# New start addresses for TensorE's operands, and single 256-column matmuls in the last SwiGLU stage

## The chip, the cores and the metric

The kernel runs on one core of a Trainium2 chip. The metric is the device time of one execution in microseconds (us), the median of several runs. TensorE (PE in the profile) multiplies; its weight loads are shown as PEld. VectorE is DVE, ScalarE is ACT, GpSimd is POOL, SyncE (SP) issues the large DMAs.

## The reference: what is computed

Sixteen meta tokens are put ahead of 256 tokens, so T = 272 rows of width D = 2048. Two layers follow, all in float32.

```python
h = concat([meta, x])                                             # 272 x 2048
h = h + short_conv_mixer(rms_norm(h), a_w_in, a_conv, a_w_out)    # 2048 -> 3*2048 -> 2048
h = h + swiglu(rms_norm(h), w_gu[0], w_down[0])                   # 2048 -> 2*5632, 5632 -> 2048
k, v, c = shared_kv(h, w_kv, w_f)                                 # keys, values, forget gate
h = h + forgetting_attention(rms_norm(h), w_q, w_o, k, v, c)      # 16 heads of 128
h = h + swiglu(rms_norm(h), w_gu[1], w_down[1])
return h[16:]                                                     # the meta rows are dropped
```

After the keys and values the meta rows are no longer needed, so from the queries on only the 256 real columns are computed.

## The kernel before, in words

The activations are kept transposed: 128 features in the partitions, the 272 (or 256) tokens along the columns. They are TensorE's **moving** operand. The weights are its stationary operand: every matmul of a 128 x 128 block of a weight matrix is preceded by the load of that block.

**Split operands.** Each float32 operand is split into two float32r parts, hi (the rounded value) and lo (the rest). A product of a weight block and an activation block is three matmuls into one PSUM accumulator: hi weights with the hi part, hi weights with the lo part, lo weights with the hi part (`mm3`, lines 101 to 103). Each of them has its own weight load.

**Slabs.** All weights stream through one list of slabs. A slab is 128 x 1024 float32 (512 KB): SP loads it into one of four `raw` buffers (line 86), ScalarE makes `whi` from it (line 95), VectorE `wlo` (line 96), each with four buffers, and TensorE then does the eight products of the slab. The main loop at the end of the kernel issues for slab i its matmuls, the split of slab i + 3, and the work that follows on finished accumulators. A slab is loaded once.

**Stages in order.** The gated convolution layer and the first SwiGLU use 272 columns (`ALL`). The attention stage mixes k and v projections (272 columns, moving operand `x`), q projections (256 columns, operands `bh` and `bl`), the work of each head (k times q, p times v, small norms, transposes) and the output projection `add_wo` (256 columns, `hid`). The last SwiGLU uses 256 columns (`REAL`).

**The last SwiGLU.** There `halves` is true (line 443): hi and lo of the moving operand lie side by side, and `product` (lines 105 to 116) does two matmuls instead of three. One has 512 columns (hi weights with hi and lo together, lines 113 and 116), the other 256 (lo weights with hi, line 114, added to the second half of the bank). The two halves of the accumulator are summed afterwards: `half_sum` by one copy on ScalarE (line 291) and one addition on VectorE (line 292), `add_residual_halves` by a copy on ScalarE (line 302), an addition on VectorE (line 303) and one on GpSimd (line 304). In the last eight blocks of products (`plain` = 14) three matmuls of 256 are used even before.

**Where operands begin.** SBUF tiles follow each other in the pools in the order in which the code makes them. What counts here is the byte address at which an operand begins, modulo 256. In the memory map of the built kernel before:

| operand | starts, bytes modulo 256 |
|---|---|
| weight buffers `raw`, `whi`, `wlo` (each 128 x 128 block is 512 bytes further) | 96 |
| `x`, `hid` with 272 columns: hi, lo | 192, 0 |
| `x`, `hid` with 256 columns: hi, lo | 224, 224 |
| `bh`, `bl` (q projection) | 224, 224 |
| p times v: moving `phi`, `plo`; weights `vhi`, `vlo` | 160; 96 |
| head norms: moving `sqh`, `sql`; weights `onesr` | 224 or 32, 96 or 160; 128 |
| k times q: moving `khi`, `klo`; weights `qhi`, `qlo` | 224 or 32, 96 or 160; 224 |

The gate of the attention stage (`gate_mm`) has the moving operands of `x` with 272 columns, and weights of 16 columns in place of 128, which begin at 224, 32, 96 and 160 in turn.

Of the kernel before, what the change touches and what calls it, by code (L numbers as in the profile page):

```python
# [9 lines left out]
F32 = mybir.dt.float32  # L10
F32R = mybir.dt.float32r
# [4 lines left out]
P = 128  # L16
NM = 16
S = 256
T = NM + S
D = 2048  # L20
KT = D // P
# [9 lines left out]
RAW_BUFS = 4  # L31
SPLIT_BUFS = 4
XROW = 640
XPAD = 24
XB = 72


@with_exitstack
def kernel(ctx, tc, x, meta, a_norm, a_w_in, a_conv, a_w_out, kv_norm, w_kv,
# [3 lines left out]
    V, A, G, PE = nc.vector, nc.scalar, nc.gpsimd, nc.tensor  # L43

    const = ctx.enter_context(tc.tile_pool(name="const", bufs=1))
    wpool = ctx.enter_context(tc.tile_pool(name="wpool", bufs=1))
    xpool = ctx.enter_context(tc.tile_pool(name="xpool", bufs=1))
    work = ctx.enter_context(tc.tile_pool(name="work", bufs=1))
    psum = ctx.enter_context(tc.tile_pool(name="psum", bufs=8, space=bass.MemoryType.PSUM))
    dram = ctx.enter_context(tc.tile_pool(name="dram", bufs=1, space=bass.MemoryType.DRAM))  # L50

    uid, late, pp = [0], [], []
    LATE = {f"b{c}{k}" for c in "hl" for k in range(KT)}
    LATE |= {"khi", "klo", "vhi", "vlo", "qhi", "qlo", "pst", "vst", "v3", "c3", "bias", "ck", "sqh", "sql"}

    def nm(s):
        uid[0] += 1
        return f"{s}_{uid[0]}"

    def wt(tag, shape, dt=F32, bufs=1):  # L60
        pool = late[0] if tag in LATE else work
        return pool.tile(shape, dt, tag=tag, name=nm(tag), bufs=bufs)

    def ps(tag):
        return psum.tile([P, 512], F32, tag="ps", name=nm(tag), bufs=8)
# [110 lines left out]
    def add_down(w, row, xs, cols, post, plain=16):  # L176

        first = None
        for pnl in range(4):
            src = w[row:row + 512, pnl * 512:(pnl + 1) * 512].rearrange("(k p) c -> p k c", p=P)  # L180
            accs = {}

            def mk(s, accs=accs, pnl=pnl):
                def mm(hi, lo):
                    for m in range(2):
                        xl = [x if pnl * 4 + s * 2 + m < plain else x[:2] + (None,) for x in xs()]
                        acc = accs[s, m] = ps("acc")
                        for k in range(4):
                            product(acc, cols, hi[:, k, m * P:(m + 1) * P],
                                    lo[:, k, m * P:(m + 1) * P], xl[k], k == 0, k == 3)  # L190
                return mm

            def mkpost(s, accs=accs, pnl=pnl):
                return lambda: [post(pnl * 4 + s * 2 + m, accs[s, m]) for m in range(2)]

            i = add_panel(src, "b", [mk(0), mk(1)], [[mkpost(0)], [mkpost(1)]])
            if first is None:
                first = i
        return first
# [4 lines left out]

    ident = const.tile([P, P], F32, name="ident")
    make_identity(nc, ident)
    ones = const.tile([P, P], F32, name="ones")
    G.memset(ones, 1.0)
    onesr = const.tile([P, P], F32R, name="onesr")
    G.tensor_copy(onesr, ones)  # L210
    epsb = const.tile([P, 1], F32, name="epsb")
    G.memset(epsb, EPS)
    small = const.tile([P, 4], F32, name="small")
# [7 lines left out]
    A.activation(warm, ones[:, 0:1], AF.Copy)  # L221


    xpool.tile([P, XPAD], F32R, name="xpad")
    state = {}

    def make_operand(key, src, gain, cols):

        k = len(state[key])
        n = cols.stop - cols.start  # L230
        at = XB if n == S else 0
        both = xpool.tile([P, XROW], F32R, tag=f"x{k}", name=nm(f"x{k}"))[:, at:]
        hi, lo = both[:, 0:n], both[:, n:2 * n]
        A.activation(hi, src, AF.Copy, scale=gain)
        V.scalar_tensor_tensor(out=lo, in0=src, scalar=gain, in1=hi.bitcast(F32),
                               op0=ALU.mult, op1=ALU.subtract)
        state[key].append((hi, lo, both[:, 0:2 * n] if 2 * n <= 512 else None))

    def add_square(k, src, cols, pool=False):
        if k == 0:  # L240
# [32 lines left out]
    def new_hidden():  # L273
        return xpool.tile([P, 4, XROW], F32R, tag="hid", name=nm("hid"), bufs=2)

    def hidden_parts(hid, k, n):
        at = XB if n == S else 0
        return hid[:, k, at:at + n], hid[:, k, at + n:at + 2 * n]

    def put_hidden(hid, k, src, n):  # L280

# [2 lines left out]
        V.tensor_tensor(out=lo, in0=src, in1=hi.bitcast(F32), op=ALU.subtract)  # L284

    def hidden_view(hid, n, both=False):
        return [hidden_parts(hid, k, n) + (hid[:, k, XB:XB + 2 * n] if both else None,) for k in range(4)]

    def half_sum(acc):
        t = wt("u", [P, T + 2], bufs=3)[:, 0:S]  # L290
        A.activation(t, acc[:, S:2 * S], AF.Copy)
        V.tensor_tensor(out=t, in0=acc[:, 0:S], in1=t, op=ALU.add)
        return t
# [64 lines left out]

    def start_done():
        start.__exit__(None, None, None)  # L360
        late.append(ctx.enter_context(tc.tile_pool(name="late", bufs=1)))
        pp.extend(late[0].tile([P, 512], F32R, name=t) for t in ("phi", "plo"))
        for t in pp:
            G.memset(t[:, 0:P].bitcast(F32), 0.0)
        G.dma_start(small[:, 0:1], k_norm.rearrange("(p o) -> p o", o=1))
        G.dma_start(small[:, 1:2], b_q_norm.rearrange("o p -> p o"))
        G.dma_start(small[0:H, 2:3], b_f.rearrange("(p o) -> p o", o=1))
        state["wf"] = wt("ck", [P, T])[:, 0:KT * H].rearrange("p (k c) -> p k c", k=KT)
        G.dma_start(state["wf"], w_f.rearrange("(k p) c -> p k c", p=P))
# [56 lines left out]
    def make_xb(m):  # L426
        if m == 0:
            state["xb"] = []
        hi = wt(f"bh{m}", [P, S], F32R)
        lo = wt(f"bl{m}", [P, S], F32R)  # L430
        t = wt("bias", [P, P + NM + T], bufs=2)[:, 0:S]
        gain = gcol[:, BN + m:BN + m + 1]
        A.activation(t, h[m][:, REAL], AF.Copy, scale=gain)
        A.activation(hi, t, AF.Copy)
        G.tensor_tensor(out=lo, in0=t, in1=hi.bitcast(F32), op=ALU.subtract)
        state["xb"].append((hi, lo, None))


    def ffn_phase(layer, cols, after):
        gu, dn = ffn_w_gu[layer], ffn_w_down[layer]  # L440
        nch = FT // 4
        n = cols.stop - cols.start
        halves = 2 * n <= 512
        plain = 14
        hid = {}
        xkey, rkey = f"xf{layer}", f"rf{layer}"
        for c in range(nch):
            col, uu = c * 512, {}

            def post_g(m, acc, uu=uu):  # L450
                r = state[rkey][:, cols]
                g = half_sum(acc) if halves else acc[:, cols]
                gs = wt("tmpa", [P, T], bufs=2)[:, 0:n]
                V.tensor_tensor(out=gs, in0=g, in1=r, op=ALU.mult)
                th = wt("tmpb", [P, T], bufs=2)[:, 0:n]
                A.activation(th, gs, AF.Tanh, scale=0.5)
                a = wt(("cs", "sc")[m // 2], [P, T], bufs=2)[:, 0:n]
                V.scalar_tensor_tensor(out=a, in0=th, scalar=1.0, in1=gs,  # L458
                                       op0=ALU.add, op1=ALU.mult)
                G.tensor_tensor(out=a, in0=a, in1=r, op=ALU.mult)  # L460
                uu[m] = a

            def post_u(m, acc, uu=uu, c=c):
                if m == 0:
                    hid[c] = new_hidden()
                u = half_sum(acc) if halves else acc[:, cols]
                z = wt("cv", [P, T], bufs=2)[:, 0:n]
                V.scalar_tensor_tensor(out=z, in0=uu[m], scalar=0.5, in1=u,
                                       op0=ALU.mult, op1=ALU.mult)
                put_hidden(hid[c], m, z, n)  # L470

            xs = lambda: state[xkey]
            if c == 0:
                hook(len(slabs) + 2, lambda: norm_stats(rkey, cols))
            add_up4(gu, col, xs, cols, post_g)
            add_up4(gu, F + col, xs, cols, post_u)
            for cc in ([c - 1] if 0 < c < nch - 1 else [c - 1, c] if c else []):
                def post_o(m, acc, cc=cc):
                    if halves and (cc < nch - 1 or m < plain):
                        add_residual_halves(m, acc, cc == nch - 1 and m >= plain - 2)  # L480
                    else:
                        add_residual(m, acc, cols)
                    if cc == nch - 1:
                        after(m)
                i = add_down(dn, cc * 512, lambda cc=cc: hidden_view(hid[cc], n, halves), cols,
                             post_o, plain if cc == nch - 1 else 16)
        return i

# [270 lines left out]
    i = ffn_phase(1, REAL, final_post)  # L759
# [52 lines left out]
```

## Time and profile before

| | |
|---|---|
| median of 3 runs | 2374.8 us (2374.6 to 2375.61) |
| the profiled execution, its own time | 2375.75 us |
| its span, first to last instruction | 2374.0 us |
| granted TensorE clock | 1.000 of full speed (2.4 GHz) |
| DMA, mean | 177 GB/s |

The profile counts an engine as busy while an instruction of it is under way. Matmuls overlap in their pipeline: a matmul of 272 columns is under way for some 288 ns, while the next one starts much sooner. What a matmul costs in a dense stream is therefore the step from its start to the next start, not its duration. In a stretch of the trace the step is the length of the stretch by the number of matmuls in it.

### The profile page before, as it was taken

Reading aid. Unit: us, or ns where it says so; the run is one execution under the profiler, and the core shown is the slowest. Engines: PE = TensorE matmul, PEld = TensorE weight load, DVE = VectorE, ACT = ScalarE, POOL = GpSimd, SP = SyncE. Lnnn points to the kernel's source line nnn. Section 1 sums busy time; section 2 is a strip of 40 time slices with the busy share of each in tenths; the row PEclk is TensorE's granted clock in tenths of the full one; section 3 lists DMA queues with packets and bytes.
Section 4 is the critical chain, followed back from the end, with each engine's and each line's share of the span. In section 5 each row is a group of like instructions: output and inputs, shape, how many; then the busy total and the mean of one; then the engine's idle time right before and its main releaser. Section 6 shows DMA issues by size and latency. Waiting matters only on the chain.

```text
span 2374.0 us, 43349 instructions
## 1 busy us (share of the span) xinstructions
PE 2366.6 (100%) x17266; PEld 2263.3 (95%) x17266; DVE 1596.4 (67%) x2350; ACT 1169.1 (49%) x1800; POOL 505.7 (21%) x585
## 2 busy tenths in 40 slices
PE   9999999999999999999999999999999999999999
PEld 8999999999999999999999999999888888888888
DVE  6665668656556566556788666778667767766677
ACT  5443345433333333333567565666555555555555
POOL 4110113000000000000265232423123223322233
PEclk9999999999999999999999999999999999999999
DMA  6555555555555555555555545545555565555554
GB/s 213 176 177 178 178 177 175 172 178 177 178 178 178 175 176 176 177 177 178 169 165 163 166 155 170 161 154 177 187 187 189 183 194 188 184 189 187 187 190 147
DMA packets 418555, 420.63 MB, mean 177 GB/s; under 512 B 13217, under 2 KB 416769, under 8 KB 418337
## 3 DMA queue, kind: packets, MB, share of 16 engines
q1 hardware_dynamic: 417280, 415.43, 54.8%
q0 software_dynamic: 1072, 2.44, 0.4%
q8 instruction: 136, 2.23, 0.4%
q14 instruction: 67, 0.54, 0.1%
HBM read 415.70 MB, written 2.11 MB: 176 GB/s over the span
## 4 chain that ended last, share of the span: by engine, by line
PE 99%; DMA 0%; DVE 0%; ACT 0%; SPq 0%; POOL 0%; issue 0%; ACTq 0%; DVEq 0%
PE acc L101 22%; PE acc L103 22%; PE acc L102 21%; PE acc L116 18%; PE acc L114 11%; PE acc L113 3%; PE aux L103 0%; PE aux L101 0%; PE aux L102 0%; PE aux L345 0%; PE aux L657 0%; PE aux L677 0%; DMA m<-in_meta_dram 0%; PE aux L546 0%; PE aux L547 0%; PE aux L750 0%
## 5 line engine op out<-in xcount | busy, mean ns | idle before, releaser
L96 DVE TENSOR_TENSOR wlo<-raw,whi 128x1024 fp32r<-128x1024 f32 x784 | 1019.6, 1301 | 646.6 <-ACT whi L95 643.2
L95 ACT ACTIVATE whi<-raw 128x1024 fp32r<-128x1024 f32 x784 | 829.4, 1058 | 917.3 <-PE acc L102 655.9
L101 PE MATMUL acc<-x,whi 128*128 128x272 f32 x2688 | 780.0, 290 | 0.0
L103 PE MATMUL acc<-x,wlo 128*128 128x272 f32 x2688 | 773.5, 288 | 0.0
L102 PE MATMUL acc<-x,whi 128*128 128x272 f32 x2688 | 772.5, 287 | 0.0
L103 PEld LDWEIGHTS acc<-x,wlo 128*128 128x128 f32 x2688 | 511.1, 190 | 0.0
L101 PEld LDWEIGHTS acc<-x,whi 128*128 128x128 f32 x2688 | 506.1, 188 | 1.4 <-ACT whi L95 0.3
L102 PEld LDWEIGHTS acc<-x,whi 128*128 128x128 f32 x2688 | 506.4, 188 | 0.1
L116 PE MATMUL acc<-x,whi 128*128 128x512 f32 x1320 | 467.1, 393 | 0.0
L114 PE MATMUL acc<-x,wlo 128*128 128x256 f32 x1408 | 383.4, 282 | 0.0
L101 PE MATMUL acc<-hid,whi 128*128 128x272 f32 (+1 forms) x1224 | 351.9, 288 | 0.0
L103 PE MATMUL acc<-hid,wlo 128*128 128x272 f32 (+1 forms) x1224 | 350.4, 286 | 0.0
L102 PE MATMUL acc<-hid,whi 128*128 128x272 f32 (+1 forms) x1224 | 349.7, 286 | 0.0
L116 PEld LDWEIGHTS acc<-x,whi 128*128 128x128 f32 x1320 | 247.9, 188 | 53.8
L114 PEld LDWEIGHTS acc<-x,wlo 128*128 128x128 f32 x1408 | 264.7, 188 | 7.6
L103 PEld LDWEIGHTS acc<-hid,wlo 128*128 128x128 f32 x1224 | 232.1, 190 | 0.1
L102 PEld LDWEIGHTS acc<-hid,whi 128*128 128x128 f32 x1224 | 230.3, 188 | 0.0
L101 PEld LDWEIGHTS acc<-hid,whi 128*128 128x128 f32 x1224 | 230.1, 188 | 0.0
L460 POOL TENSOR_TENSOR cs<-cs,rstd 128x272 f32<-128x272 f32 (+1 forms) x44 | 33.3, 757 | 899.6 <-DVE cs L458 899.6
L304 POOL TENSOR_TENSOR h<-h,u 128x256 f32<-128x256 f32 x172 | 156.3, 934 | 269.0 <-DVE h L303 269.0
L116 PE MATMUL acc<-hid,whi 128*128 128x512 f32 x522 | 190.6, 394 | 0.0
L114 PE MATMUL acc<-hid,wlo 128*128 128x256 f32 x696 | 167.7, 281 | 0.0
(194 smaller groups left out, 2379.3 us busy)
## 6 DMA issues: line engine op xcount, KB each, us to landing
raw<-in_ffn_w_gu_dram SPq DMA_DIRECT2D x352, 512.0 KB, 3.5
raw<-in_ffn_w_down_dram SPq DMA_DIRECT2D x176, 512.0 KB, 3.3
raw<-in_a_w_in_dram SPq DMA_DIRECT2D x96, 512.0 KB, 3.6
raw<-in_w_kv_dram SPq DMA_DIRECT2D x64, 512.0 KB, 3.7
raw<-in_a_w_out_dram SPq DMA_DIRECT2D x32, 512.0 KB, 4.4
raw<-in_b_w_q_dram SPq DMA_DIRECT2D x32, 512.0 KB, 3.3
raw<-in_b_w_o_dram SPq DMA_DIRECT2D x32, 512.0 KB, 3.3
ck<-cdram POOLq DMA_DIRECT2D x16, 136.0 KB, 3.9
```

The costliest lines, as they stand in the source:

```text
L95: A.activation(hi, part, AF.Copy)
L96: V.tensor_tensor(out=lo, in0=part, in1=hi.bitcast(F32), op=ALU.subtract)
L101: PE.matmul(acc, whi, xhi, start=first, stop=False)
L102: PE.matmul(acc, whi, xlo, start=False, stop=False)
L103: PE.matmul(acc, wlo, xhi, start=False, stop=last)
L113: PE.matmul(acc, whi, both, start=True, stop=False)
L114: PE.matmul(acc[:, S:2 * S], wlo, xhi, start=False, stop=False)
L116: PE.matmul(acc, whi, both, start=False, stop=last)
L304: G.tensor_tensor(out=h[m][:, REAL], in0=h[m][:, REAL], in1=t, op=ALU.add)
L460: G.tensor_tensor(out=a, in0=a, in1=r, op=ALU.mult)
```

## The change

It moves operands in SBUF and takes the 512-column matmuls away.

```diff
-XPAD = 24
-XB = 72
+XLO = 320
+WPAD, XPAD, BPAD = 40, 48, 8
...
+    wpool.tile([P, WPAD], F32, name="wpad")
+    xpool.tile([P, XPAD], F32R, name="xpad")
...
-    ones = const.tile([P, P], F32, name="ones")
+    onesr = const.tile([P, P], F32R, name="onesr")
+    ones = onesr.bitcast(F32)
     G.memset(ones, 1.0)
-    onesr = const.tile([P, P], F32R, name="onesr")
-    G.tensor_copy(onesr, ones)
...
+    def halves(n):
+
+        return False
...
-        at = XB if n == S else 0
-        both = xpool.tile([P, XROW], F32R, tag=f"x{k}", name=nm(f"x{k}"))[:, at:]
-        hi, lo = both[:, 0:n], both[:, n:2 * n]
+        both = xpool.tile([P, XROW], F32R, tag=f"x{k}", name=nm(f"x{k}"))
+        at = S if halves(n) else XLO
+        hi, lo = both[:, 0:n], both[:, at:at + n]
...
     def hidden_parts(hid, k, n):
-        at = XB if n == S else 0
-        return hid[:, k, at:at + n], hid[:, k, at + n:at + 2 * n]
+        at = S if halves(n) else XLO
+        return hid[:, k, 0:n], hid[:, k, at:at + n]
...
+        bpool.append(ctx.enter_context(tc.tile_pool(name="bpool", bufs=1)))
+        bpool[0].tile([P, BPAD], F32R, name="bpad")
...
-        hi = wt(f"bh{m}", [P, S], F32R)
-        lo = wt(f"bl{m}", [P, S], F32R)
+        hi, lo = (bpool[0].tile([P, S], F32R, tag=f"b{c}{m}", name=nm(f"b{c}{m}")) for c in "hl")
...
-        halves = 2 * n <= 512
+        pair = halves(n)
...
-                g = half_sum(acc) if halves else acc[:, cols]
+                g = half_sum(acc) if pair else acc[:, cols]
```

The same replacement of `halves` by `pair` (now always false) is made in `post_u`, in `post_o` and in the views of `hid`. By the sizes in the code the starts become, modulo 256: the constants lose one tile of 512 bytes, `wpad` adds 160 bytes to 96, so the weight buffers begin at 0; the twelve buffers take 49,152 bytes, a multiple of 256, and `xpad` adds 192; rows of 640 elements are 2,560 bytes and lo begins 1,280 bytes behind hi, both multiples of 256. So `x`, `hid`, `bh`, `bl`, `phi` and `plo` all begin at 192. The operands of the heads move to multiples of 64: `khi` 0 or 64, `klo` 128 or 192, `qhi` and `qlo` 0, `vhi` and `vlo` 128, `sqh` 0 or 64, `sql` 128 or 192; `onesr` stays at 128.

## Rows read from the trace of the kernel before

**Rows 1.** Page, part 1: busy us (share of the span) xinstructions, whole execution.

```profile
PE 2366.6 (100%) x17266; PEld 2263.3 (95%) x17266; DVE 1596.4 (67%) x2350; ACT 1169.1 (49%) x1800; POOL 505.7 (21%) x585
```

**Rows 2.** Page, part 4: chain of waits that ended last, by engine.

```profile
PE 99%; DMA 0%; DVE 0%; ACT 0%; SPq 0%; POOL 0%; issue 0%; ACTq 0%; DVEq 0%
```

**Rows 3.** Windows: first SwiGLU, last SwiGLU, the start. Busy us (xinstructions), PEclk, DMA, GB/s.

```profile
core 0: us, PE busy (x) PEld busy (x) DVE busy (x) ACT busy (x) POOL busy (x), PEclk, DMA share, GB/s
430.00:1190.00 760.00, 760.00 (x6109) 760.00 (x6108) 461.54 (x607) 309.76 (x377) 48.76 (x57) 1.00 0.55 176
1650.00:2350.00 700.00, 700.00 (x3992) 612.36 (x3991) 497.09 (x669) 370.10 (x584) 190.63 (x205) 1.00 0.59 188
5.00:43.00 38.00, 36.64 (x245) 33.37 (x245) 24.65 (x37) 24.55 (x48) 22.38 (x27) 1.00 0.76 239
```

**Rows 4.** Windows of the last SwiGLU: instructions of line 116, then of line 113.

```profile
1650.00:2350.00 700.00, 623.56 (x1748) 328.05 (x1748) 1.00 0.59 188
...
1650.00:2350.00 700.00, 97.76 (x247) 46.31 (x247) 1.00 0.59 188
```

**Rows 5.** Groups by line and form, PE, whole execution: xcount, busy us, mean ns.

```profile
L101 PE MATMUL acc<-x,whi 128*128 128x272 f32 x2688 | 780.0, 290 | 0.0
...
L116 PE MATMUL acc<-x,whi 128*128 128x512 f32 x1320 | 467.1, 393 | 0.0
...
L101 PE MATMUL acc<-hid,whi 128*128 128x272 f32 x960 | 277.4, 289 | 0.0
...
L116 PE MATMUL acc<-hid,whi 128*128 128x512 f32 x522 | 190.6, 394 | 0.0
...
L101 PE MATMUL acc<-hid,whi 128*128 128x256 f32 x264 | 74.5, 284 | 0.0
...
L101 PE MATMUL acc<-bh,whi 128*128 128x256 f32 x256 | 72.6, 284 | 0.0
...
L113 PE MATMUL acc<-hid,whi 128*128 128x512 f32 x174 | 69.2, 398 | 0.0
L113 PE MATMUL acc<-x,whi 128*128 128x512 f32 x88 | 34.8, 395 | 0.0
```

**Rows 6.** Timeline, merged, line 101 in an output projection: durations min/median/max, first and last start.

```profile
L101 PE MATMUL acc<-hid,whi x64: 279/281/285, 1318.2 to 1340.6; 128*128 128x256 f32 x64
```

**Rows 7.** Timeline of PE in the gate's matmuls: start us, us; the first and the 22nd.

```profile
1223.10 0.29 PE L101 MATMUL aux<-x,sqh 128*16 128x272 f32 x1
...
1225.71 0.29 PE L101 MATMUL aux<-x,sqh 128*16 128x272 f32 x1
```

**Rows 8.** Timeline of PE, p times v of one head: first and last of six.

```profile
1266.94 0.28 PE L101 MATMUL aux<-phi,vhi 128*128 128x256 f32 x1
...
1267.53 0.28 PE L103 MATMUL aux<-phi,vlo 128*128 128x256 f32 x1
```

**Rows 9.** Timeline of PE at head norms: each matmul and the one behind it.

```profile
1311.76 0.28 PE L546 MATMUL aux<-sqh,onesr 128*128 128x256 f32 x1
1311.87 0.28 PE L547 MATMUL aux<-sql,onesr 128*128 128x256 f32 x1
...
1361.34 0.28 PE L546 MATMUL aux<-sqh,onesr 128*128 128x272 f32 x1
1361.46 0.28 PE L101 MATMUL acc<-bh,whi 128*128 128x256 f32 x1
...
1362.17 0.30 PE L547 MATMUL aux<-sql,onesr 128*128 128x272 f32 x1
1362.31 0.28 PE L101 MATMUL acc<-bh,whi 128*128 128x256 f32 x1
```

**Rows 10.** Groups by line, 1650 to 2350 us: busy us, mean ns, idle before and its releaser.

```profile
L304 POOL TENSOR_TENSOR h<-h,u 128x256 f32<-128x256 f32 x162 | 149.1, 946 | 260.6 <-DVE h L303 260.6
...
L302 ACT ACTIVATE u<-acc 128x256 f32<-128x256 f32 x164 | 63.1, 385 | 84.5 <-PE acc L116 79.7
...
L291 ACT ACTIVATE u<-acc 128x256 f32<-128x256 f32 x84 | 32.2, 383 | 41.1 <-PE acc L116 41.1
```

**Rows 11.** Chain of waits in order of time: the longest piece at the start.

```profile
1.74 4.84 DMA m<-in_meta_dram
```

More of the change, by code (lines that the diff above doesn't have):

```diff
@@ L48 @@
     work = ctx.enter_context(tc.tile_pool(name="work", bufs=1))
+    wpool.tile([P, WPAD], F32, name="wpad")
+    xpool.tile([P, XPAD], F32R, name="xpad")
     psum = ctx.enter_context(tc.tile_pool(name="psum", bufs=8, space=bass.MemoryType.PSUM))
     dram = ctx.enter_context(tc.tile_pool(name="dram", bufs=1, space=bass.MemoryType.DRAM))
-    uid, late, pp = [0], [], []
-    LATE = {f"b{c}{k}" for c in "hl" for k in range(KT)}
-    LATE |= {"khi", "klo", "vhi", "vlo", "qhi", "qlo", "pst", "vst", "v3", "c3", "bias", "ck", "sqh", "sql"}
+    uid, late, pp, bpool = [0], [], [], []
+    LATE = {"khi", "klo", "vhi", "vlo", "qhi", "qlo", "pst", "vst", "v3", "c3", "bias", "ck", "sqh", "sql"}
     def nm(s):
@@ L221 @@
     A.activation(warm, ones[:, 0:1], AF.Copy)
-    xpool.tile([P, XPAD], F32R, name="xpad")
     state = {}
+    def halves(n):
+        return False
     def make_operand(key, src, gain, cols):
@@ L236, in make_operand @@
                                op0=ALU.mult, op1=ALU.subtract)
-        state[key].append((hi, lo, both[:, 0:2 * n] if 2 * n <= 512 else None))
+        state[key].append((hi, lo, both[:, 0:2 * n] if halves(n) else None))
     def add_square(k, src, cols, pool=False):
@@ L286, in hidden_view @@
     def hidden_view(hid, n, both=False):
-        return [hidden_parts(hid, k, n) + (hid[:, k, XB:XB + 2 * n] if both else None,) for k in range(4)]
+        return [hidden_parts(hid, k, n) + (hid[:, k, 0:2 * n] if both else None,) for k in range(4)]
     def half_sum(acc):
@@ L465, in post_u @@
                     hid[c] = new_hidden()
-                u = half_sum(acc) if halves else acc[:, cols]
+                u = half_sum(acc) if pair else acc[:, cols]
                 z = wt("cv", [P, T], bufs=2)[:, 0:n]
@@ L478, in post_o @@
                 def post_o(m, acc, cc=cc):
-                    if halves and (cc < nch - 1 or m < plain):
+                    if pair and (cc < nch - 1 or m < plain):
                         add_residual_halves(m, acc, cc == nch - 1 and m >= plain - 2)
@@ L484, in post_o @@
                         after(m)
-                i = add_down(dn, cc * 512, lambda cc=cc: hidden_view(hid[cc], n, halves), cols,
+                i = add_down(dn, cc * 512, lambda cc=cc: hidden_view(hid[cc], n, pair), cols,
                              post_o, plain if cc == nch - 1 else 16)
```

## The prediction, on record before the changed kernel ran

> **What bounds the kernel now.** I read the page's busy times first: PE is under way for 2366.6 us of a 2374.0 us span, the next engine, DVE, for 67% of it [rows 1]. A busy PE need not be a PE that sets the end, so the chain of waits comes second: it lies 99% on PE [rows 2]. The windows of the two SwiGLU stages come third: PE is busy in every microsecond, at a granted clock of 1.00 (the upper level, 2.4 GHz), while DVE, ACT and DMA have a quarter or more to spare [rows 3]. So the time is a number of matmuls by the step from one start to the next, and only what changes the count or the step matters.
>
> The steps. In the first SwiGLU 6,109 matmuls touch 760 us; one lasts 290 ns [rows 5], so two had begun before, and 760 us / 6,107 is **124.4 ns** for 272 columns. At one column per cycle of 2.4 GHz it would be 113.3, so 11.1 ns are lost at each. In the output projection 63 triples of 256 columns take 1318.2 to 1340.6 us [rows 6]: 22.4 us / 189 is **118.5 ns**, against 106.7 (11.8 lost). In the last SwiGLU 700 us hold 1,748 + 247 = 1,995 products [rows 4]: **350.9 ns** for a 512 and a 256. The losses add up to about a tenth of the kernel, and the change can only work on them.
>
> **The change part by part.** Its parts are the new starts for the 272-column stages, the same for the 256-column matmuls of attention, two matmuls turned into three in the last SwiGLU, and what falls away on other engines.
>
> *What the starts can do.* The trace has no pair of a moving operand at 192 and weights at 0, so I bound the step from both sides by the same shapes at other starts. At 256 columns the six matmuls of p times v (moving 160, weights 96) go from 1266.94 to 1267.53 in five steps, 118.0 ns each [rows 8]. A head norm (moving 32, next weights at 128) steps 0.11 us [rows 9]; that stamp is good to 0.01, and I read it as 112 to 116. At 272 columns one norm matmul (moving 32, next weights at 96, which is 192 modulo 256 behind, the distance that the change gives everywhere) steps 0.12 us and another (moving 160, next weights 96) 0.14 [rows 9]. So starts do move the step, by several ns and in both directions. What speaks for little at 272 is the gate: its weights have 16 columns in place of 128, and 21 steps from 1223.10 to 1225.71 still take 124.3 ns [rows 7]. If weight reads in the way of moving reads made the whole loss, an eighth of the weights should have made less of it.
>
> *272 columns.* The count is 3 x (2,688 + 960) = 10,944 [rows 5]. Bounds of the new step: 120 below, 132 above (the 0.12 and the low side of 0.14, rounded). I take 123.2, about a quarter of the way from 124.4 to 120: nearest to the thousands of matmuls of the stage and to the gate, a little down for the one row with the distance of the change. 10,944 x 1.2 = **-13.1 us**.
>
> *256 columns in attention.* 3 x (256 + 264) less 24 in the last blocks of the last SwiGLU is 1,536 [rows 5]. Bounds 112 and 122 (the same 3.5 above as the norm lies below its 118.5 at 115). I take 116, between p times v and the norm. 1,536 x 2.5 = **-3.8 us**.
>
> *The last SwiGLU.* 1,320 + 522 + 174 + 88 = 2,104 products [rows 5] go from 350.9 ns to three matmuls of 256. At 116 that is 348.0, so 2,104 x 2.9 = **-6.1 us**; at the step of today it would be 355.5 and a loss of 9.7 us; at the bounds 336 (-31 us) and 366 (+32 us). The break-even is 117.0 ns. The added weight load per product is hidden under the matmul before it as the others are: in the first SwiGLU as many loads as matmuls run at 124.4 ns a step [rows 3].
>
> *What falls away.* In 700 us of that stage the copies on ACT take 63.1 + 32.2 us and the additions on POOL 149.1 us [rows 10]; one DVE addition per block remains. All of it runs beside a PE that is busy throughout [rows 3], so it is costed at nothing; were PE not the cover, it would be a relief and no price. The copy of the ones at the start goes too; there the kernel waits 4.84 us for the meta tokens [rows 11], so nothing again. No wait, no DMA and no step of the order is added: the `b` tiles only lie in a pool of their own. Slabs are used up to 1% sooner, 188 GB/s becoming about 190, while the start moved 239 [rows 3]; DMA stays hidden.
>
> *The sum.* -13.1 - 3.8 - 6.1 = -23.0 us against the profiled execution's own 2375.75 us (1.75 us of it lie outside the span) gives 2352.8; that execution is 0.95 us over the median of the runs shown, so I say **2351.8 us**, and 2335 to 2365 if this reading is right.
>
> **The rivals.**
>
> *Much more comes back* (2286 us). If 192 against 0 keeps the two streams of reads out of each other's way for a whole matmul, 272 columns go at 120 and 256 at 112: -10,944 x 4.4 - 1,536 x 6.5 - 2,104 x (350.9 - 336.0) = -48 - 10 - 31 = -89. For it: these steps do occur [rows 9], and after the change every matmul has the same pair of starts, so a good pair is good 17,000 times. Against it: they occur singly, and the gate's step with short weights is no shorter than the stage's [rows 7].
>
> *Starts make no difference* (2384.5 us, **slower**). Then 272 and 256 columns keep their steps and only the split of the 512s is left: 2,104 x (3 x 118.5 - 350.9) = +9.7 us. It decides as soon as the new 256-column step is over 117.0 ns. For it: the gate, and p times v with another start at 118.0 [rows 7, 8]. Against it: the 0.11 and 0.14 us of the norms [rows 9].
>
> Beside this rival stands a rule: the Trainium skill, SBUF — State Buffer, section "Who interferes with whom", gives PE two independent read ports, one for the moving operand and one for weights, and says that PE never waits on anyone. By that rule starts have no effect and this rival is the outcome; the trace agrees with it in the gate and disagrees in the norms. Another page, TensorE: Matmul & The Clock Gate, section "Back-to-back issue gap", has columns by 2.4 plus 2.5 ns, which is 109.2 for 256 columns and 215.8 for 512; by it three matmuls against a 512 and a 256 would cost 2.6 ns more per product, an estimate of +5 us. The trace has 118.5 where it says 109.2, so the rule lacks a loss of some 9 ns.
>
> *The pair is a bad one* (about 2460 us, slower). The same regularity can hurt: where 272 columns at 160 are followed by weights at 96, the step is 0.14 us [rows 9]; at 132 for all of them, 10,944 x 7.6 = +83 us. One row shows it, at another distance than the change makes.
>
> *The change does not do what it says* only in small: the operands of the heads get multiples of 64, not 192 and 0. They are under 2% of the matmuls.
>
> **How the numbers follow.** About 0.2% (4.7 us) is what a measurement of this kernel can tell from no change. I give my forecast 0.48, the larger gain 0.19, starts without effect 0.18, the bad pair 0.06, and 0.09 to a small gain at 272 columns that the split of the 512s eats up (within 0.2%). Faster is 0.48 + 0.19 = 0.67, same 0.09, slower 0.18 + 0.06 = 0.24. The range reaches from 2290 (most of the larger gain) to 2388 (starts without effect, and 3 us of an uneven step beside it); it leaves out the bad pair and about half of the larger gain.
>
> **What would show it.** Right: in the first SwiGLU about 6,170 matmuls in 760 us instead of 6,109; in the output projection 63 triples in 21.9 us instead of 22.4; in the last SwiGLU about 2,010 products in 700 us, each of three matmuls, with POOL's busy time there down by about 149 us and no gap on PE. Wrong: an unchanged 124.4 ns at 272 columns (then the loss isn't one of starts), a step over 117.0 at 256 (then the split of the 512s costs), or PE waiting for `whi`, `wlo` or a free accumulator in the last stage (then another engine has become the bound).

## The result, and the profile after

The changed kernel takes **2335.6 us** (2334.88 to 2336.14, 4 runs) against 2375.2 us before (2374.6 to 2376.09, 4 runs): ratio 0.9833, 95% interval 0.9816 to 0.985. It is 39.6 us faster. The forecast was 2351.8, so the direction holds, the size was too small, and the time lies inside the range.

The page of the changed kernel, busy times, then the chain of waits by engine:

```profile
PE 2326.6 (100%) x19370; PEld 2315.8 (99%) x19370; DVE 1525.6 (65%) x2260; ACT 1085.4 (46%) x1540; POOL 352.8 (15%) x412
...
PE 97%; DVE 1%; issue 1%; POOL 1%; DMA 0%; ACT 0%; SPq 0%; POOLq 0%; ACTq 0%
```

PE still sets the end, with 2,104 matmuls more than before [rows 1, 2] in 40 us less. So the step from start to start has become shorter. Windows of the changed kernel, first and last SwiGLU (busy us with the number of instructions, by engine):

```profile
430.00:1190.00 760.00, 760.00 (x6162) 759.92 (x6162) 469.57 (x617) 317.72 (x392) 57.08 (x63) 1.00 0.55 178
1650.00:2300.00 650.00, 650.00 (x5738) 650.00 (x5737) 410.49 (x561) 279.63 (x324) 39.95 (x40) 1.00 0.61 194
```

Of the matmuls that touch a window, two had begun before it. At 272 columns the step is 760 us / 6,160 = **123.4 ns** (124.4 before [rows 3]). At 256 columns it is 650 us / 5,736 = **113.3 ns**, so a product of three is 340.0 ns against 350.9 for a 512 and a 256 before [rows 4]. POOL's work in the stage has shrunk from 190.63 us in 700 [rows 3] to 40 in 650, and PE has no gap before or after: that work was indeed beside the path. The granted clock is 1.00 in both kernels.

The output projection of the changed kernel, the timeline merged for line 102 (the first of the three matmuls; line 101 before), says something else:

```profile
L102 PE MATMUL acc<-hid,whi x64: 278/281/281, 1306.5 to 1328.7; 128*128 128x256 f32 x64
```

Here 63 triples take 22.2 us, 117.5 ns a matmul, hardly less than the 118.5 before [rows 6]. It has the same width, the same starts and the same lines of code as the last SwiGLU, and a step that is 4 ns longer. The experiments come back to this.

All steps from one start to the next, added up by stage, give where the time went. The last SwiGLU behind its norm went from 734.1 to 710.9 us (-23.2). The matmuls of 272 columns in all stages take 12.4 us less, and the 256s of attention some 5 (119.9 to 116.8 ns on average, with the steps around other work in between). Together that is about the 40 us.

### The profile page after: what moved, and what is told of

The parts are those of the page before. It is cut to its first block, busy times and chain, and to the rows that moved or that the text cites. A ratio compares the mean times of both kernels' runs of the same rounds, so it can differ in the third digit from the quotient of the medians.

```text
span 2334.4 us, 46907 instructions
## 1 busy us (share of the span) xinstructions
PE 2326.6 (100%) x19370; PEld 2315.8 (99%) x19370; DVE 1525.6 (65%) x2260; ACT 1085.4 (46%) x1540; POOL 352.8 (15%) x412
## 4 chain that ended last, share of the span: by engine, by line
PE 97%; DVE 1%; issue 1%; POOL 1%; DMA 0%; ACT 0%; SPq 0%; POOLq 0%; ACTq 0%
PE acc L102 31%; PE acc L104 31%; PE acc L103 31%; PE aux L104 0%; PE aux L103 0%; PE aux L348 0%; PE aux L102 0%; DVE wlo L97 0%; PE aux L661 0%; DVE x L238 0%; PE aux L681 0%; DMA m<-in_meta_dram 0%; POOL cv L562 0%; PE aux L754 0%; PE aux L663 0%
## 5 line engine op out<-in xcount | busy, mean ns | idle before, releaser
L102 PE MATMUL acc<-x,whi 128*128 128x272 f32 (+1 forms) x4096 | 1162.2, 284 | 0.0
L103 PE MATMUL acc<-x,whi 128*128 128x272 f32 (+1 forms) x4096 | 1160.0, 283 | 0.0
L104 PE MATMUL acc<-x,wlo 128*128 128x272 f32 (+1 forms) x4096 | 1159.6, 283 | 0.0
L102 PEld LDWEIGHTS acc<-x,whi 128*128 128x128 f32 x4096 | 771.5, 188 | 1.4 <-ACT whi L96 0.3
L103 PEld LDWEIGHTS acc<-x,whi 128*128 128x128 f32 x4096 | 771.4, 188 | 0.1
L102 PE MATMUL acc<-hid,whi 128*128 128x272 f32 (+1 forms) x1920 | 541.3, 282 | 0.0
L104 PE MATMUL acc<-hid,wlo 128*128 128x272 f32 (+1 forms) x1920 | 540.8, 282 | 0.0
L103 PE MATMUL acc<-hid,whi 128*128 128x272 f32 (+1 forms) x1920 | 540.7, 282 | 0.0
L102 PEld LDWEIGHTS acc<-hid,whi 128*128 128x128 f32 x1920 | 361.5, 188 | 0.0
L104 PEld LDWEIGHTS acc<-hid,wlo 128*128 128x128 f32 x1920 | 361.1, 188 | 0.1
L103 PEld LDWEIGHTS acc<-hid,whi 128*128 128x128 f32 x1920 | 361.1, 188 | 0.0
L310 DVE TENSOR_TENSOR h<-h,acc 128x272 f32<-128x272 f32 (+1 forms) x480 | 203.0, 424 | 66.1 <-PE acc L104 62.1
L102 PE MATMUL acc<-bh,whi 128*128 128x256 f32 x256 | 71.8, 281 | 0.0
L103 PE MATMUL acc<-bl,whi 128*128 128x256 f32 x256 | 71.1, 278 | 0.0
```

The costliest lines, as they stand in the source:

```text
L102: PE.matmul(acc, whi, xhi, start=first, stop=False)
L103: PE.matmul(acc, whi, xlo, start=False, stop=False)
L104: PE.matmul(acc, wlo, xhi, start=False, stop=last)
L310: V.tensor_tensor(out=h[m][:, cols], in0=h[m][:, cols], in1=acc[:, cols], op=ALU.add)
```

## The experiments

Each is compared with the kernel before, run on the same chip beside it (2374.6 to 2375.7 us). Steps named "mean" are means over all matmuls of a group whose neighbours have the same width, steps over 160 ns left out. A "row" is an unbroken run of products of one width, without such a longer step and without other matmuls in it.

### The split alone, and the starts alone

**old_starts_three**: the kernel before with three matmuls of 256.

```diff
-        halves = 2 * n <= 512
+        halves = False
...
-        state[key].append((hi, lo, both[:, 0:2 * n] if 2 * n <= 512 else None))
+        state[key].append((hi, lo, None))
```

> The split alone: starts of the kernel before, but three matmuls of 256 in the whole last SwiGLU. If the starts made the gain, the 256-column step stays at 118.5 ns, a product costs 355.5 instead of 350.9, and the time is 2375.2 + 9.7 = 2385 us. If the shape made the gain (fewer copies and additions behind it, no 512-column matmul), the step falls to the 113.5 of the changed kernel, a product to 340, and the time is about 2352 us.

Measured: 2386.99 us, ratio 1.0047 (1.0032 to 1.0062), 11.3 us slower than before. The last SwiGLU:

```profile
1650.00:2300.00 650.00, 650.00 (x5480) 650.00 (x5479) 392.75 (x527) 265.64 (x306) 29.66 (x39) 1.00 0.60 186
```

650 us / 5,478 is 118.7 ns. The shape brings nothing; alone it costs. The rival of the prediction in which starts make no difference (+9.7 us) is thereby priced by a run: it is what the split costs without the new starts.

**new_starts_pair**: the changed kernel with 512 and 256 per product.

```diff
     def halves(n):
 
-        return False
+        return 2 * n <= 512
```

> The starts alone: those of the changed kernel, but a 512 and a 256 per product in the last SwiGLU as before. If the starts made the gain, the 256 goes at 113.5 ns and the 512 at some 225 (113.5 for the part beside a weight load, 111.7 for the rest, which is 231.6 - 119.9 of before): 338.5 per product against 340.5 for three, so about 2332 us. If the shape made it, a product is back at 350.9 and the time at 2335.6 + 2104 x 10.4 = 2357 us.

Measured: 2359.66 us, ratio 0.9933 (0.9918 to 0.9948). In the last SwiGLU the 512s step 234 ns and the 256s 118 on average: 352 per product, the price of before. So neither part alone gives the whole gain. The starts give 16 us without the split, by the 272 columns and the attention stage; the split then gives 24 us more, while at the old starts it costs 11. My expectation of 225 ns for a 512 was wrong.

### Distance or multiples of 64

**all_plus32** and **weights_128**: the changed kernel with other pads.

```diff
-WPAD, XPAD, BPAD = 40, 48, 8
+WPAD, XPAD, BPAD = 48, 48, 8
```

```diff
-WPAD, XPAD, BPAD = 40, 48, 8
+WPAD, XPAD, BPAD = 72, 16, 8
```

In the first the weights begin at 32 and the moving parts at 224 modulo 256, in the second the weights at 128 and the moving parts at 192.

> The changed kernel with every operand 32 bytes further: weights at 32, moving parts at 224 modulo 256. If the distance of the two starts decides (192 as in the changed kernel), steps stay at 123.4 and 113.5 ns and the time at 2336 us. If it is the multiples of 64, both are off them now and the steps go back to 124.5 and 118.5: 2335.6 + 10,944 x 1.1 + 7,872 x 5.0 = 2387 us.

> The changed kernel with the weight buffers at 128 in place of 0, moving parts still at 192: all on multiples of 64, distance 64 instead of 192. If the multiples of 64 decide, steps stay at 123.4 and 113.5 ns and the time at 2336 us. If the distance decides, the 256-column step is that of p times v before, which had distance 64: 118.0; with 124.5 at 272 columns the time is 2335.6 + 10,944 x 1.1 + 7,872 x 4.5 = 2383 us.

Measured: all_plus32 2337.54 us (0.9841; 0.9826 to 0.9855), weights_128 2401.81 us (1.0111; 1.0094 to 1.0127). The windows of all_plus32, then of weights_128:

```profile
430.00:1190.00 760.00, 760.00 (x6163) 759.92 (x6162) 469.86 (x616) 317.62 (x392) 57.07 (x63) 1.00 0.57 178
1650.00:2300.00 650.00, 650.00 (x5738) 650.00 (x5737) 410.68 (x561) 279.66 (x324) 39.91 (x40) 1.00 0.63 194
```

```profile
430.00:1190.00 760.00, 760.00 (x6002) 760.00 (x6001) 446.30 (x586) 294.99 (x339) 34.32 (x44) 1.00 0.56 174
1650.00:2300.00 650.00, 650.00 (x5519) 649.95 (x5519) 404.08 (x549) 271.85 (x315) 34.50 (x43) 1.00 0.61 188
```

With everything off the multiples of 64 but at the same distance, the counts are those of the changed kernel to within one. With everything on multiples of 64 but at distance 64, 272 columns take 126.7 ns and the long row of 256 columns 117.8, and the kernel is slower than before. So "on multiples of 64" is no part of the gain. At 272 columns the distance between the moving part and the weights decides: every row at distance 64 is near 126.6 ns. At 256 columns it is not the whole story. The trace of weights_128 has three short rows at 113.3 to 113.4 ns. One is in the third output projection; the next row of that projection is as long and has the same starts (first and last matmul of both, 46 steps each):

```profile
1605.67 0.28 PE L103 MATMUL acc<-hid,whi 128*128 128x256 f32 x1
...
1610.88 0.28 PE L104 MATMUL acc<-hid,wlo 128*128 128x256 f32 x1
...
1611.67 0.28 PE L103 MATMUL acc<-hid,whi 128*128 128x256 f32 x1
...
1617.08 0.28 PE L104 MATMUL acc<-hid,wlo 128*128 128x256 f32 x1
```

5.21 us against 5.41 us: 113.3 against 117.6 ns a step. So distance 64 has the short step at 256 columns too, though seldom, and that its long row goes at 117.8 is not shown to be the work of the distance.

### Which distances

**sweep_a to sweep_d**: the changed kernel with an offset of its own for each group of matmuls, weights at 0. For sweep_c:

```diff
+XAT = {272: 8, 256: 8}
+HAT = {272: 4, 256: 4}
...
-        at = S if halves(n) else XLO
-        hi, lo = both[:, 0:n], both[:, at:at + n]
+        at = XAT[n]
+        hi, lo = both[:, at:at + n], both[:, XLO + at:XLO + at + n]
```

(and the same in `hidden_parts` with `HAT`; one element is 4 bytes; a pad moves `bh` and `bl`, and in sweep_d another one `x` and `hid`).

> The changed kernel with the weights at 0 and the moving parts at other distances, one per group of matmuls: x at 0 and hid at 32 modulo 256 (272 and 256 columns both), bh and bl at 96. If the step depends smoothly on the distance (best near 192, worst near 64), 272 columns take some 125 ns and 256 columns some 116: 2335.6 + 10,944 x 1.6 + 7,872 x 2.5 = 2373 us. If 192 is one lucky value among equals, all the others are at 124.5 and 118.5 and the time is 2387 us.

> As sweep_a with other distances: x at 96 for both widths, hid at 128 with 272 columns and at 160 with 256, bh and bl at 224. Smooth dependence: 272 columns at 125.5 ns, 256 columns at 118 for x and 116 for the others: 2335.6 + 10,944 x 2.1 + 4,224 x 4.6 + 3,648 x 2.6 = 2388 us, the differences in the steps of the groups. One lucky value: 124.5 and 118.5 in all groups, 2387 us.

> As sweep_a close to the changed kernel on one side: x at 224, hid at 208, bh and bl at 192. Smooth dependence: 16 and 32 bytes away cost a part of the way only, some 0.3 and 0.6 ns at 272 columns, 0.8 and 1.6 at 256: 2350 us. One lucky value: 124.5 and 118.5 for x and hid at once, 2383 us.

> As sweep_a close to the changed kernel on the other side: x at 160 with 272 columns and 176 with 256, hid at 176 with 272 and 200 with 256, bh and bl at 128. Smooth dependence: steps within 0.6 ns of 123.4 and 0.8 of 113.4 but for bh and bl (118.5): 2351 us. One lucky value: 124.5 and 118.5 in all groups, 2387 us.

Measured, one run each: 2399.81, 2410.39, 2406.48 and 2384.46 us. The mean steps in ns, by distance (start of the moving part less start of the weights, modulo 256), with those of the runs above; at distance 192 and 256 columns, the last SwiGLU alone:

| distance | 272 columns | 256 columns |
|---|---|---|
| 0 | 125.3 | 120.0 |
| 32 | 125.7 | 117.6 |
| 64 | 126.6 | 117.8 |
| 96 | 126.5 | 120.0 |
| 128 | 126.6 | 118.8 |
| 160 | 123.5 | 117.8 |
| 176 | 123.4 | 119.3 |
| **192** | **123.4** | **113.3** |
| 200 | not tried | 121.0 |
| 208 | 126.7 | 119.2 |
| 224 | 126.5 | 118.3 |

Windows of sweep_c, the convolution stage (x at 224, hid at 208) and the last SwiGLU:

```profile
60.00:340.00 280.00, 280.00 (x2213) 280.00 (x2212) 165.78 (x205) 108.37 (x120) 33.74 (x42) 1.00 0.56 173
1670.00:2330.00 660.00, 660.00 (x5568) 660.00 (x5567) 398.98 (x537) 270.77 (x313) 32.20 (x41) 1.00 0.60 185
```

280 us / 2,211 is 126.6 ns: 16 bytes past the start of the changed kernel already cost 3.3 ns a matmul. The smooth curve is refuted. At 272 columns the three distances from 160 to 192 are a shelf at 123.4 to 123.5 and the rest is at 125.3 to 126.7, so "lucky value among equals" does not fit there. The kernel before, with hi at distance 96 and lo at 160, had 124.4, better than 96 alone at 126.5.

At 256 columns 192 stands alone in the table among 117.6 to 121.0, and 8 bytes beside it lie at 121.0. But the table has means, and rows can differ. I count rows of 20 matmuls and more, without their first six steps, in the traces of all runs on record, those of the next sections too, wherever a group has one distance only:

| distance | rows | settle at 113.3 to 113.4 | settle at 117.7 to 117.9 | others |
|---|---|---|---|---|
| 192 | 221 | 151 | 70 | none |
| 64 | 39 | 3 | 36 | none |
| the nine others | 203 | none | 2 | 201, from 116.6 to 121.7 |

So 192 and 64 are alike in having two steps and nothing between. What differs is how often each occurs. At the other distances no row comes under 116.6; for 0 and 176 there is only one row each.

### Whose weights, and can parts differ

**wlo_64**: the lo weights begin at 64, the lo parts of x and hid at 0 modulo 256.

```diff
-WPAD, XPAD, BPAD = 40, 48, 8
+WPAD, XPAD, BPAD = 40, 32, 8
...
+        if i == 0:
+            wpool.tile([P, 16], F32, name="lpad")
...
+XAT = {272: (0, 336), 256: (0, 336)}
+HAT = {272: (0, 336), 256: (0, 336)}
...
-        at = S if halves(n) else XLO
-        hi, lo = both[:, 0:n], both[:, at:at + n]
+        at, lat = XAT[n]
+        hi, lo = both[:, at:at + n], both[:, lat:lat + n]
```

The pairs are where hi and lo begin in their row, in elements; `HAT` does the same for hid.

> Which weights count, those of a matmul itself or those loaded while it runs? The lo weights begin at 64 modulo 256, the hi weights stay at 0; of x and hid the hi part begins at 192, the lo part at 0. Against the weights loaded beside it (those of the next matmul) every matmul of x and hid then has the distance 192; against its own weights only one in three has (the others 0 and 128). If the next weights count, steps stay at 123.4 and 113.4 ns and only bl, left at 192, loses: 2337 us. If the own weights count, two of three matmuls take what those distances took, 120.0 and 118.8 ns at 256 columns and 125.3 and 126.6 at 272: 2335.6 + 3,648 x 5.1 + 2,368 x 12 = 2383 us. If equal starts of all moving parts were the point, they are gone too and the time is about 2380.

Measured: 2395.57 us, ratio 1.0087 (1.0058 to 1.0117). Mean steps are 125.5 ns at 272 and 118.5 at 256 columns. Windows of the convolution stage and the last SwiGLU:

```profile
60.00:340.00 280.00, 280.00 (x2233) 280.00 (x2232) 168.82 (x209) 110.18 (x121) 36.68 (x45) 1.00 0.56 174
1670.00:2330.00 660.00, 660.00 (x5571) 660.00 (x5571) 398.84 (x537) 271.00 (x313) 29.82 (x40) 1.00 0.60 186
```

Distance 192 to the weights that load beside a matmul is not enough. Whether its own weights must fit too, or all moving parts must begin alike, this run doesn't tell apart.

**mix_a** and **mix_b**: weights all at 0, hi and lo at different starts (the offsets of `XAT` and `HAT` as pairs).

> Weights all at 0; hi and lo parts at different starts: x with 272 columns 192 and 160, hid with 272 columns 160 and 192, x with 256 columns 192 and 64, hid with 256 columns 192 and 0. If each matmul has the price of its own distance, the step is the mean of one lo and two hi prices: 123.4 in both groups of 272, 114.8 for x and 115.5 for hid at 256: 2335.6 + 4,224 x 1.4 + 2,880 x 2.1 = 2348 us. If the short step is a rhythm that all matmuls of a row must share, the 256s fall back to about 118: 2335.6 + 7,104 x 4.5 = 2368 us.

> As mix_a: x with 272 columns 192 and 0, hid with 272 columns 192 and 64, x with 256 columns 192 and 160, hid with 256 columns 160 and 192. Prices by distance: (2 x 123.4 + 125.3) / 3 = 124.0 and 124.5 at 272 columns, 114.8 and 116.3 at 256: 2335.6 + 8,064 x 0.65 + 2,880 x 1.1 + 4,224 x 1.45 + 2,880 x 2.9 = 2358 us. A shared rhythm: 118 at 256 columns and 124.4 at 272, about 2378 us.

Measured, one run each: 2387.3 and 2375.9 us. Mean steps over the three matmuls of a product: mix_a 125.6 (192 and 160) and 124.5 (160 and 192) at 272 columns, 117.8 (192 and 64) and 118.3 (192 and 0) at 256; mix_b 124.5 and 124.4, 117.8 and 117.9. The prices by distance would have given 123.4 to 124.5 and 114.8 to 116.3. So a matmul has no price of its own by its distance: at 272 columns mix_a refutes it (125.6 ns where the prices give 123.4), at 256 columns those at 192 whose next weights lie at 0 take 116 to 119 ns in such a row, and no row of x or hid settles at 113. The time of mix_a is 19 us over even the expectation of a shared rhythm, because its 272s became slower as well.

### What runs ahead of the row

What remained was the output projection of the changed kernel at 117.5 ns, with the right starts. Its row follows matmuls of 272 columns directly. The long row of the last SwiGLU runs behind a norm. The q projections of the changed kernel give a hint. Each has four slabs with the same two accumulators, the same `bh` and `bl` and the same starts. In all eight of them the row of the first slab directly follows 272-column matmuls of x and settles at 117.8 ns; the rows of the later slabs, behind work of the heads or the gate, settle at 113.3 to 113.4. First and last matmul of the first and of the fourth slab of one projection (23 steps each):

```profile
1279.12 0.28 PE L102 MATMUL acc<-bh,whi 128*128 128x256 f32 x1
...
1281.83 0.28 PE L104 MATMUL acc<-bh,wlo 128*128 128x256 f32 x1
...
1290.18 0.28 PE L102 MATMUL acc<-bh,whi 128*128 128x256 f32 x1
...
1292.80 0.28 PE L104 MATMUL acc<-bh,wlo 128*128 128x256 f32 x1
```

That is 2.71 us against 2.62 us.

**entry_272**: twelve spare matmuls of 272 columns behind that norm.

```diff
+    def entry_run():
+        klo, qhi = heads[15]["k"][1], heads[15]["q"][0]
+        acc = ps("aux")
+        for i in range(12):
+            PE.matmul(acc[:, ALL], qhi[:, 0:P], klo, start=i == 0, stop=i == 11)
...
                 hook(len(slabs) + 2, lambda: norm_stats(rkey, cols))
+                if layer == 1:
+                    hook(len(slabs) + 2, entry_run)
```

> The changed kernel with twelve spare matmuls of 272 columns (moving part at 192, weights at 0, result unused) behind the norm at the beginning of the last SwiGLU, so that its long row of 256-column matmuls begins behind 272-column ones, as the output projections do, and not behind the norm. The spare matmuls cost 12 x 123.4 ns = 1.5 us. If the starts alone decide, the row keeps 113.4 ns and the time is 2337 us. If the starts only allow the short rhythm and what runs ahead of the row decides whether it is entered, the row goes at the 117.8 ns of those output projections: 2335.6 + 1.5 + 6,100 x 4.4 = 2364 us.

Measured: 2365.21 us (2364.74 to 2365.55), ratio 0.9957 (0.994 to 0.9973). That is 29.6 us more than the changed kernel, for 1.5 us of matmuls. The timeline of PE where the row begins, first in the changed kernel, then in entry_272 (start us, us, engine, line):

```profile
1615.62 0.28 PE L103 MATMUL acc<-x,whi 128*128 128x256 f32 x1
1615.73 0.28 PE L104 MATMUL acc<-x,wlo 128*128 128x256 f32 x1
1616.11 0.70 PE L268 MATMUL aux<-sqacc,onesr 128*128 128x256 f32 x2
1616.46 0.47 PE L102 MATMUL acc<-x,whi 128*128 128x256 f32 x1
1616.76 0.28 PE L103 MATMUL acc<-x,whi 128*128 128x256 f32 x1
```

```profile
1616.19 0.70 PE L268 MATMUL aux<-sqacc,onesr 128*128 128x256 f32 x2
1616.54 1.83 PE L447 MATMUL aux<-klo,qhi 128*128 128x272 f32 x12
1618.21 0.28 PE L102 MATMUL acc<-x,whi 128*128 128x256 f32 x1
1618.33 0.28 PE L103 MATMUL acc<-x,whi 128*128 128x256 f32 x1
1618.45 0.28 PE L104 MATMUL acc<-x,wlo 128*128 128x256 f32 x1
```

And the windows of entry_272 further on:

```profile
430.00:1190.00 760.00, 760.00 (x6163) 759.92 (x6162) 469.98 (x617) 319.60 (x392) 57.07 (x63) 1.00 0.58 178
1650.00:2300.00 650.00, 650.00 (x5521) 650.00 (x5520) 396.82 (x534) 268.86 (x311) 29.77 (x40) 1.00 0.61 187
```

In the first SwiGLU nothing differs. In the last, 650 us / 5,519 is 117.8 ns, although every matmul there has the operands, the starts and the order of the changed kernel: the whole row of some 6,100 runs at the longer step, to its end. The spare matmuls also take one accumulator, so the later ones lie one PSUM buffer further; that this decides is not likely, because the q projections above show both steps with the same two accumulators. The steps of the last SwiGLU add up to 738.0 us against 710.9, so 27.1 us, and the spare matmuls take 1.5: 28.6 of the 29.6 us. So at 256 columns the starts only allow the short **rhythm**, as I call a step that a row settles into and keeps; how the row is entered decides whether it is taken, and it then persists. In the changed kernel and in all_plus32 each of the 11 rows directly behind 272-column matmuls of x with weights of 128 columns has the longer rhythm. "Behind 272 columns" is not a rule by itself: rows behind a head norm of 272 columns, or behind the gate (272 columns of x, weights of 16 columns, at 1218 us), come down to 113 ns after some steps, and in mix_a and mix_b, where the lo part of x begins elsewhere, all eight first slabs of the q projections settle at 113.3. Nor is a pause: of the six short rows at the end of the changed kernel, all behind a step of some 0.2 us, four settle at 113.3 to 113.4 and two at 117.8.

The entry also fits to all_plus32 being 1.9 us slower than the changed kernel. Its q projections take 2.0 us more, and 13 of their short rows, behind a head norm or k times q, settle at 117.7 to 117.8 in place of 113.3 to 113.4. Their own distance is the same, but the ones of the head norm lie ahead of the pad and were not moved.

## Why the prediction was right, and where its sizes were off

**What bounds the kernel** was right. PE is busy throughout, and the time is the number of matmuls by the step. What was costed at nothing (copies, additions, the extra weight loads, DMA at 194 GB/s) cost nothing.

**272 columns** were right almost to the digit: 123.2 forecast, 123.4 measured; -13.1 us forecast, -12.4 found. The reason given was in part luck. I leaned on one norm row [rows 9] with the distance of the change, and the sweep shows that the distance 192 does stand well, but on a shelf with 160 and 176 and not as the nearest of a smooth family.

**256 columns in attention** were right in size and by luck: 116 forecast, a mean of 115.4 measured (118.8 before, steps over 160 ns left out), -3.8 us against some -5. No settled row goes at 116: the mean is that of rows at 113.3 and at 117.8.

**The last SwiGLU** is the term that was mis-sized: -6.1 us forecast, -23.2 measured. The step that failed is "at 116 that is 348.0". I took one step for all 256-column matmuls, half-way between p times v and a norm; the stage measured 113.3, near the lower bound of 112. What I had not considered is that a row of equal matmuls can settle into one of two rhythms and keep it for 700 us. Which one it took here was luck as well: in entry_272, with the same starts, the step is 117.8, over the prediction's break-even of 117.0, and a product takes 353.4 ns, more than the 350.9 of before. The argument for the larger gain had the seed of it ("every matmul has the same pair of starts, so a good pair is good 17,000 times"), but read it as a property of the pair alone.

**The rivals.** Starts without effect: refuted by weights_128, which moves nothing but the weights and is 66 us slower than the changed kernel. About 36 of them are the 272 columns, which have one step for each distance (10,944 x 3.3 ns); the others are the long row and attention at 256, where the entry has a part. The price of that rival was right, +9.7 against 11.3 measured with the old starts. The larger gain came true at 256 columns in the last stage (113.3 against 112) and not at 272 (123.4 against 120). A bad pair exists, but a milder one than the 132 ns of the rival: 126.7 at 272 columns and distance 64, the distance of the 0.14 us norm that the rival rested on [rows 9].

**The rules weighed there.** The Trainium skill, SBUF — State Buffer, section "Who interferes with whom", lets PE never wait on anyone, with two independent read ports. By that rule weights_128 and the changed kernel take the same time; the runs have 2401.8 and 2335.6 us, so the measurement decides against an outcome without effect, for float32r matmuls. Whether reads in each other's way are the reason is not shown. The Trainium skill, TensorE: Matmul & The Clock Gate, section "Back-to-back issue gap", gives columns by 2.4 plus 2.5 ns as the gap of an isolated matmul, which is 109.2 ns for 256 columns. No row here settles under 113.3.

**What stays open.** What in the chip makes the rhythm was not shown: only that it hangs on the distance of the starts modulo 256 and on the entry. What it is in the entry that decides is open too. With distance 64 no run tried to bring the long row into the short rhythm, so at 256 columns 64 is not shown to be worse than 192. Another entry ahead of the output projections that now run at 117.8 ns (two and a quarter of the four) wasn't tried. Their 432 matmuls by some 4 ns would give about 1.9 us, and the first slabs of the q projections 0.9 us. No version faster than the changed kernel was found.

## What to carry to other kernels

When PE is busy all the time, compare the step between matmul starts with columns by 2.4 GHz before looking at other engines, and compare it between rows of equal shape: a few ns at 19,000 matmuls are 40 us. Where an operand begins, relative to the weights and modulo 256 bytes, can be such a few ns, so change the start addresses in one run per distance and read the steps by row, not only their mean: the mean of 115.4 ns in attention was a mixture of 113.3 and 117.8. And repeat the reading after every change of order: an address that pays today can stop paying because of a dozen matmuls in front of the row.

## What the runs showed of the hardware that was not expected

The same stream of 256-column float32r matmuls, with the same start addresses, runs at 113.3 or at 117.8 ns a matmul for hundreds of microseconds, and the matmuls just before it decide which (2335.6 against 2365.2 us). Both steps occur at the distances 192 (151 and 70 rows) and 64 (3 and 36 rows), the short one at no other distance tried. Moving the moving part by 8 bytes, from distance 192 to 200, brings 121.0 ns. Moving weights and moving parts by 32 bytes together changes nothing in the long rows (5,738 matmuls in 650 us both times).
